# A two-layer hybrid attention kernel on one core: scores on 128 rows with stacked queries and doubled keys, norm steps in PSUM, stacked mixing weights

## The chip, the cores and the metric

The kernel runs on one core of one Trainium2 chip. Time is the device time of one execution in microseconds (us); the figure used is the median of several timed runs. A separate execution is recorded by the hardware profiler, and all rows of profiles come from that one. TensorE is called PE in the profile (its weight loads PEld), VectorE DVE, ScalarE ACT, GpSimd POOL, SyncE SP.

## The reference

512 tokens of width 1024 pass through two layers and a final RMS norm, all in float32. A layer, cut to what matters:

```python
h = rmsnorm(x, norm_g)                       # x * rsqrt(mean(x*x) + 1e-6) * g
proj = h @ w_in                              # all of what follows is a column range of proj
ya = moba_attention(rope(a_q), rope(a_k), a_v) * silu(a_g)         # 6 heads of 64, causal
yb = dsa_attention(rope(b_q), rope(b_k), b_v, rope(i_q), rope(i_k), i_w) * silu(b_g)
yc = dilated_mixture(rope(c_q), rope(c_k), c_v) * silu(c_g)        # 3 groups of 4 heads
merged = gate0 * (ya @ w_br_a) + gate1 * (yb @ w_br_b) + gate2 * (yc @ w_br_c)
x = x + merged @ w_out
```

Branch A (moba) is causal softmax attention at this length. Branch B (dsa) has six query heads over one key head, and attends for each token only to the 128 keys whose index score is highest; the index score is a weighted sum over four index heads of relu(iq . ik). Branch C has three groups of four heads with strides 1, 4 and 16; each group is attention within a band, and the three results of a head are mixed with weights from a softmax over their log-sum-exps.

## The kernel before, in words

**Products.** Every float32 product is made of three passes on TensorE. An operand is split into a high part (a cast on ScalarE) and a low part (a subtraction, on POOL for weights, tile `wlo`, line L326, and for operands from SBUF; on VectorE, L379, for operands from PSUM), and the passes are high x high, low x high and high x low. The projections (`t_block` L406, `n_block` L426) are such passes of 128 rows and up to 512 columns: lines L417 to L419 and L436 to L438.

**What sets the order.** The kernel first lists all its operations (`add`, L66), each with its engine, an assumed cost, the tiles that it reads and writes and a priority. `Plan.schedule` (L105) then lists them: at each step it takes, on the engine that can begin first, the operation that can begin first, and among those the one of the lowest priority number. A tile comes from a pool with a fixed number of slots by tag (for example two PSUM tiles for scores, "sc", and one, "pv", for the products with the values), and an operation that needs a new tile waits until a slot is free. Projections and branch products are "fill" (`pe_fill`, L339): they keep the order in which they are listed. Attention work has a lower priority number, so it goes ahead of fill as soon as its operands are there, and fill lies between its steps. The units of a layer are listed in the order of the string `ORDER` (L27): values, index, keys, top-k, queries, the branches' attention, gates, branch products. DMA transfers, weights and copies alike, are issued by SP's queue in the order of the plan (`dma`, L273).

**Queries and keys.** `rope_group` (L442) projects four heads at a time to 128-row tiles X and Y (the even and odd halves of four heads), rotates them on VectorE and POOL into tiles `rt`, and copies them by DMA to z tiles (`zq`, `zk`, `zn`, `zc` and so on), where two heads lie below one another, each on 64 rows. `split_pair` (L480) splits a z tile: a cast of 128x512 on ScalarE and a subtraction of 128x512 on POOL.

**Scores.** `scores` (L505) makes a block of scores, 128 queries by N keys (N is 128 to 512) of two heads: three products for two heads, six matmuls, each on 64 rows. The two heads of a pair use the two halves of the rows, and are issued one behind the other. There are 76 such blocks in the two layers: index (`topk`, L764), A and B (`attend`, L554) and group 0 of C (`c_group0`, L873). Groups 1 and 2 of C have their own code (L951, their scores in L963). `soft` (L520) and what follows it in `attend` make the softmax: mask, exponential and sum, reciprocal, the scaling by it (ScalarE, L586), transposes on TensorE (L591), the split, and the products with the values (`pv`, L614 and L626).

**Norm.** `square` (L636) sums the squares of a row tile (128 tokens) in four pieces, `rstd` (L705) makes 1/rms of it with four tiny VectorE steps on 128x1 or 128x4 (L712, L714 to L716) and a square root on ScalarE, all in one SBUF tile `sq`. `norm_tile` (L680) scales x by it and by the gain (`h`, L687; in layer 0 the gain is a PSUM tile `gp`, in layer 1 an SBUF tile `gb`), and TensorE transposes the result (`tpn`, L693). The final norm uses `rstd` too.

**Mixing.** `c_mix` (L1019) makes the weights of the three groups, transposes them to 12 rows, and splits them into `rh` and `rl`. For each of two head pairs and three groups a tile `bc` (L1057) spreads the weights of two heads over 128 rows: two matmuls of 12 rows, `sel` being a matrix of zeros and ones.

## Time and profile before

| | |
|---|---|
| median of 3 runs | 1096.1 us (1096.06 to 1096.89) |
| profiled execution, its own time | 1097.91 us |
| its span, first to last instruction | 1096.1 us |
| mean granted TensorE clock | 0.998 |
| instructions | 17334 |

The span is shorter than the profiled execution's own time by 1.8 us, which lie before its first and behind its last instruction. In the profile's rows a duration is that of one instruction as the profiler gives it; matmuls are pipelined, so that one begins before the row of the last has ended. A row of TensorE in the timeline that ends in "x2" stands for two matmuls that run side by side. In groups of instructions, what follows the second bar is the engine's idle time just before them, with what ended it.

### The profile page before, as it was taken

Reading aid. Unit: us, or ns where it says so; the run is one execution under the profiler, and the core shown is the slowest. Engines: PE = TensorE matmul, PEld = TensorE weight load, DVE = VectorE, ACT = ScalarE, POOL = GpSimd, SP = SyncE. Lnnn points to the kernel's source line nnn. Section 1 sums busy time; section 2 is a strip of 40 time slices with the busy share of each in tenths; the row PEclk is TensorE's granted clock in tenths of the full one; section 3 lists DMA queues with packets and bytes.
Section 4 is the critical chain, followed back from the end, with each engine's and each line's share of the span. In section 5 each row is a group of like instructions: output and inputs, shape, how many; then the busy total and the mean of one; then the engine's idle time right before and its main releaser. Section 6 shows DMA issues by size and latency. Waiting matters only on the chain.

```text
span 1096.1 us, 17334 instructions
## 1 busy us (share of the span) xinstructions
PE 1085.4 (99%) x5746; PEld 885.2 (81%) x5746; DVE 490.6 (45%) x1416; ACT 574.3 (52%) x1466; POOL 644.0 (59%) x656
## 2 busy tenths in 40 slices
PE   9999999999999999999999999999999999999997
PEld 5887887778878887888978788777888887778887
DVE  6127885465445313113351388755644452221144
ACT  5534336687767653334353343467876775532432
POOL 4764765654544637876566277565653455396853
PEclk9999999999999999999999999999999999999999
DMA  6642543523222332353654144434422224235322
GB/s 222 180 109 63 140 107 92 147 75 82 73 68 78 97 81 76 106 173 97 188 161 134 30 116 116 111 90 123 114 66 63 67 80 108 78 87 177 120 79 78
DMA packets 112596, 116.40 MB, mean 106 GB/s; under 512 B 17773, under 2 KB 94457, under 8 KB 112506
## 3 DMA queue, kind: packets, MB, share of 16 engines
q1 hardware_dynamic: 112216, 114.97, 37.8%
q8 instruction: 45, 0.74, 0.3%
q14 instruction: 45, 0.37, 0.1%
q10 hardware_dynamic: 290, 0.33, 0.1%
HBM read 96.06 MB, written 6.36 MB: 93 GB/s over the span
## 4 chain that ended last, share of the span: by engine, by line
PE 48%; DMA 1%; POOL 1%; issue 1%; ACT 1%; DVE 0%; SPq 0%; ACTq 0%
PE pp L417 11%; PE pp L419 11%; PE pp L418 11%; PE sc L515 2%; PE pp L436 2%; PE pp L438 1%; PE pp L437 1%; PE po L1112 1%; PE po L1111 1%; PE po L1110 1%; PE tp L591 1%; DMA ws<-in_w_in_dram 1%; PE pv L614 1%; PE pv L626 1%; POOL wlo L326 1%
## 5 line engine op out<-in xcount | busy, mean ns | idle before, releaser
L326 POOL TENSOR_TENSOR wlo<-ws,whi 128x256 fp32r<-128x256 f32 (+2 forms) x439 | 438.5, 1013 | 321.5 <-ACT whi L320 255.1
L417 PE MATMUL pp<-h_hi,whi 128*128 128x512 f32 (+1 forms) x896 | 361.8, 404 | 0.0
L419 PE MATMUL pp<-h_hi,wlo 128*128 128x512 f32 (+1 forms) x896 | 348.6, 389 | 0.0
L418 PE MATMUL pp<-h_lo,whi 128*128 128x512 f32 (+1 forms) x896 | 348.3, 389 | 0.0
L320 ACT CAST whi<-ws 128x512 fp32r<-128x512 f32 (+2 forms) x434 | 213.2, 507 | 250.0 <-PE pp L418 130.7
L417 PEld LDWEIGHTS pp<-h_hi,whi 128*128 128x128 f32 x896 | 168.4, 188 | 41.5 <-issue 7.4
L419 PEld LDWEIGHTS pp<-h_hi,wlo 128*128 128x128 f32 x896 | 168.2, 188 | 35.7
L418 PEld LDWEIGHTS pp<-h_lo,whi 128*128 128x128 f32 x896 | 168.7, 188 | 28.8
L379 DVE TENSOR_TENSOR ptl<-tp,pth 128x256 fp32r<-128x256 f32 (+3 forms) x128 | 58.0, 462 | 47.2 <-ACT pth L320 46.6
L847 DVE SCALAR_TENSOR_TENSOR th<-th,pp 128x512 f32<-128x512 f32 x32 | 22.0, 688 | 109.6 <-PE pp L419 106.7
L436 PE MATMUL pp<-whi,h_hi 128*128 128x512 f32 (+2 forms) x192 | 68.0, 354 | 0.0
L438 PE MATMUL pp<-whi,h_lo 128*128 128x512 f32 (+2 forms) x192 | 66.7, 348 | 0.0
L437 PE MATMUL pp<-wlo,h_hi 128*128 128x512 f32 (+2 forms) x192 | 66.7, 347 | 0.0
L320 ACT CAST pth<-tp 128x256 fp32r<-128x256 f32 (+3 forms) x128 | 50.3, 405 | 28.7 <-PE tp L591 18.2
L1110 PE MATMUL po<-whi,mhh 128*128 128x256 f32 (+1 forms) x192 | 61.4, 320 | 0.0
L1111 PE MATMUL po<-wlo,mhh 128*128 128x256 f32 (+1 forms) x192 | 61.1, 318 | 0.0
L1112 PE MATMUL po<-whi,mhl 128*128 128x256 f32 (+1 forms) x192 | 61.1, 318 | 0.0
L525 ACT ACTIVATE p<-p,st 128x128 f32<-128x128 f32 (+3 forms) x96 | 53.6, 559 | 3.1 <-DVE st L523 3.1
L832 ACT ACTIVATE th<-pp 128x512 f32<-128x512 f32 x48 | 28.6, 595 | 50.5 <-PE pp L419 50.3
L586 ACT ACTIVATE p<-p,st 128x128 f32<-128x128 f32 (+3 forms) x96 | 51.7, 558 | 1.9 <-DVE st L585 1.7
L417 PE MATMUL pp<-yh,whi 128*128 128x512 f32 x128 | 51.7, 404 | 0.0
L793 DVE MATCH_REPLACE8 work<-m,work 128x512 f32<-128x512 f32 (+2 forms) x96 | 51.6, 542 | 0.0
(198 smaller groups left out, 1718.4 us busy)
## 6 DMA issues: line engine op xcount, KB each, us to landing
ws<-in_w_in_dram SPq DMA_DIRECT2D x232, 256.0 KB, 2.9
ws<-in_w_out_dram SPq DMA_DIRECT2D x32, 256.0 KB, 2.7
ws<-in_w_in_dram SPq DMA_DIRECT2D x24, 192.0 KB, 2.8
zq<-rt SPq DMA_DIRECT2D x32, 128.0 KB, 2.8
x<-x SPq DMA_DIRECT2D x16, 256.0 KB, 3.5
x<-in_x_dram SPq DMA_DIRECT2D x15, 256.0 KB, 4.2
vd<-vn SPq DMA_DIRECT2D x8, 256.0 KB, 3.4
ws<-in_w_in_dram SPq DMA_DIRECT2D x16, 128.0 KB, 2.3
```

The lines of the kernel that those rows point to most:

```text
L320: add("act", n_act(n), lambda: nc.scalar.copy(dst(), src()), r=r, w=w, pri=pri, name=name, alt=("dve", n_dve(n, two), lambda: nc.vector.te ...
L326: add("pool", n_pool(n), lambda: nc.gpsimd.tensor_tensor(dst(), a(), b(), op), r=r, w=w, pri=pri, name=name, alt=("dve", n_dve(n), lambda: ...
L379: add("dve", n_dve(n), lambda: nc.vector.tensor_tensor(lo_fn(), src_fn(), hi_fn().bitcast(F32), ALU.subtract), r=[src, hi], w=[lo], pri=pr ...
L417: nc.tensor.matmul(o, lhs(hi.t, k % 2), a, start=(k == 0), stop=False)
L418: nc.tensor.matmul(o, lhs(hi.t, k % 2), b, start=False, stop=False)
L419: nc.tensor.matmul(o, lhs(lo.t, k % 2), a, start=False, stop=(k == nk - 1))
L436: nc.tensor.matmul(ps.t[:, :width], tokfn(h_hi, k), hi.t[:, kk, :width], start=(k == 0), stop=False)
L437: nc.tensor.matmul(ps.t[:, :width], tokfn(h_hi, k), lo.t[:, kk, :width], start=False, stop=False)
L438: nc.tensor.matmul(ps.t[:, :width], tokfn(h_lo, k), hi.t[:, kk, :width], start=False, stop=(k == KD - 1))
L1110: nc.tensor.matmul(ps.t[:, :n], mh.t[:, c], hi.t[:, kk, :n], start=(k == 0), stop=False)
L1111: nc.tensor.matmul(ps.t[:, :n], mh.t[:, c], lo.t[:, kk, :n], start=False, stop=False)
L1112: nc.tensor.matmul(ps.t[:, :n], ml.t[:, c], hi.t[:, kk, :n], start=False, stop=(k == KD - 1))
```

## The change

**Scores.** A query tile now holds one head: the high part on 64 rows and the low part on the other 64 (`split_heads`: a cast of 64x512 on ScalarE and a subtraction of 64x512 on VectorE for each head). A key tile holds one key head twice, on rows 0 to 63 and 64 to 127, and is split into high and low as before. Then the doubled key high part against the stacked query gives two products in one pass of 128 rows, and the doubled key low part against it gives the third, and low x low beside it. `scores` makes four matmuls of 128 rows where it made six of 64. It holds for the index, A, B and group 0 of C; groups 1 and 2 of C keep their 64 rows.

**Units.** Since the keys of A and of C's group 0 are stored twice, their rotation works on a pair of query heads and the same pair's key heads (`qk_a(p)`, `c_qk0(p)`), with a column of scale factors `scol` (-0.125 on the queries' rows, 1 on the keys') in place of one number or none. `twice` writes each key head by DMA to both halves of its tile, in pieces of 32 rows. The attention of A, B and C's group 0 is listed by pair (AA0 to AA2, AB0 to AB2, C00, C01), the rotations by pair (A0 to A2, D0, D1), C's group 0 values by themselves (CW), and `ORDER` is a new string.

**Norm.** The sums of squares of all four row tiles lie in one PSUM tile of tag "pv" (`Part` is eight columns of it). The tiny steps read it, and their results lie in an SBUF tile `rstd`. In layer 1 ScalarE writes the gain to PSUM tiles. The warm-up matmuls use the tag "pp". The four memsets of `sq` on POOL are one on VectorE in each layer's norm.

**Mixing.** High and low weights lie in one tile `rw` of 64 rows (rows 0 to 11 and 32 to 43, POOL sets the others to zero), `sel` has its ones on both, and `bc` is one matmul of 64 rows.

In all, over the whole program, TensorE has 5476 matmuls for 5640, VectorE 38 instructions more, ScalarE 35 more, POOL 20 fewer, and SP 672 transfers for 569.

The diff, cut to its core (`attend` loses its loop over pairs and is otherwise only moved to the left):

```diff
-ORDER = "CV I K V Q T gA C0 gB A AB VR AA C1 gC B1 C2 B0 MX B2"
+ORDER = "CV K I V Q D0 D1 A1 CW T gC C01 gA C00 gB A0 AB0 AB1 AB2 AA0 AA1 VR C1 A2 AA2 B1 C2 B0 MX B2"
...
+class Part:
+    def __init__(self, buf, at, tok):
+        self.buf, self.at, self.tok = buf, at, tok
+    @property
+    def t(self):
+        return self.buf.t[:, self.at:self.at + 8]
...
-        dma(lambda g=g, s32=s32: s32.t[4 * g:4 * g + 4], lambda: k_sel[32:36], s32, 300, pri=50)
+        for p0 in (4 * g, 32 + 4 * g):
+            dma(lambda s32=s32, p0=p0: s32.t[p0:p0 + 4], lambda: k_sel[32:36], s32, 300, pri=50)
...
-    warm = buf("pv", [P, T], F32, "warm")
+    warm = buf("pp", [P, T], F32, "warm")
...
+    def split_heads(z, name, t0=0):
+        out_ = []
+        pri = -5e4 + fill[1] + 0.5
+        n = T - t0
+        for f in range(2):
+            b = buf("u", [P, T], FR, name)
+            r, o = slice(64 * f, 64 * f + 64), slice(64 - 64 * f, 128 - 64 * f)
+            copy(n, lambda b=b, r=r: b.t[r, t0:], lambda r=r: z.t[r, t0:], [z], [b], pri, "hi", True)
+            add("dve", n_dve(n), lambda b=b, r=r, o=o: nc.vector.tensor_tensor(b.t[o, t0:], z.t[r, t0:], b.t[r, t0:].bitcast(F32), ALU.subtract),
+                r=[z], w=[b], pri=pri, name="lo", port=True)
+            out_.append(b)
+        return out_
...
     def scores(qp, kp, i, N, koff, name):
-        (qh, ql), (kh, kl) = qp, kp
         sc = [buf("sc", [P, T], F32, "sc") for _ in range(2)]
         pri = apri()
         def fn():
-            for n, (a, b) in enumerate(((qh, kh), (ql, kh), (qh, kl))):
-                for f in range(2):
-                    r = slice(64 * f, 64 * f + 64)
-                    nc.tensor.matmul(sc[f].t[:, :N], a.t[r, i * P:(i + 1) * P], b.t[r, koff:koff + N],
-                                     start=(n == 0), stop=(n == 2))
-        add("pe", n_pair(6, N), fn, r=[qh, ql, kh, kl], w=sc, pri=pri, name=name)
+            for f in range(2):
+                for n in range(2):
+                    nc.tensor.matmul(sc[f].t[:, :N], qp[f].t[:, i * P:(i + 1) * P], kp[f][n].t[:, koff:koff + N],
+                                     start=(n == 0), stop=(n == 1))
+        add("pe", n_mm(4, N), fn, r=[*qp, *kp[0], *kp[1]], w=sc, pri=pri, name=name)
         return sc, pri
...
-            sq[t] = buf("st", [P, 8], F32, "sq")
-            add("pool", 70, lambda st=sq[t]: nc.gpsimd.memset(st.t[:, 0:4], 0.0), w=[sq[t]], pri=-5e5, after=() if wide else plan.ops[-1:])
+            if t == 0:
+                stats[0] = buf("pv", [P, 32], F32, "sq")
+                add("dve", 80, lambda b=stats[0]: nc.vector.memset(b.t, 0.0), w=[stats[0]], pri=-5e5, after=() if wide else plan.ops[-1:])
+            sq[t] = Part(stats[0], 8 * t, token(f"sq{t}"))
...
+    def load_g(src, to_psum=False):
         g = [buf("u", [P, T], F32, "gb") for _ in range(2)]
         for b in range(2):
             dma(lambda b=b: g[b].t, lambda b=b: src[:, b * T:(b + 1) * T].to_broadcast([P, T]), g[b], 725, pri=-2e5, after=fills[-30:-29])
+        o = [buf("sc", [P, T], F32, "gp") for _ in range(2)] if to_psum else g
         for b in range(2):
-            add("act", n_act(T), lambda b=b: nc.scalar.activation(g[b].t, g[b].t, AF.Copy, scale=-0.5), r=[g[b]], w=[g[b]], pri=-2e5, name="gb",
-                alt=("dve", n_dve(T, True), lambda b=b: nc.vector.tensor_scalar(g[b].t, g[b].t, -0.5, None, op0=ALU.mult), 0.0), port=True)
-        return g
+            add("act", n_act(T), lambda b=b: nc.scalar.activation(o[b].t, g[b].t, AF.Copy, scale=-0.5), r=[g[b]], w=[o[b]], pri=-2e5, name="gb")
+        return o
...
-        st = sq[t]
-        rstd(st, pri)
+        st = rstd(sq[t], pri)
...
-                h.t[:, c], xb.t, st.t[:, 7:8], gb.t, op0=ALU.mult, op1=ALU.mult), r=[xs[t][b], st, gb[b]], w=[h], pri=pri, name="hn", port=port)
+                h.t[:, c], xb.t, st.t[:, 1:2], gb.t, op0=ALU.mult, op1=ALU.mult), r=[xs[t][b], st, gb[b]], w=[h], pri=pri, name="hn")
...
     def rstd(st, pri):
         c = lambda n: st.t[:, n:n + 1]
         stt = nc.vector.scalar_tensor_tensor
-        def tiny(fn, r=()):
-            add("dve", 80, fn, r=[st, *r], w=[st], pri=pri, name="tiny")
+        r = buf("st", [P, 8], F32, "rstd")
+        def tiny(fn, reads=(), w=None):
+            add("dve", 120, fn, r=[st.buf, *reads], w=[st.tok if w is None else w], pri=pri, name="tiny")
         tiny(lambda: nc.vector.tensor_tensor_reduce(st.t[:, 0:4], st.t[:, 0:4], invd.t, 1.0, EPS, ALU.mult, ALU.add, c(4)), [invd])
-        add("act", 250, lambda: nc.scalar.activation(c(5), c(4), AF.Sqrt), r=[st], w=[st], pri=pri, name="sqrt")
-        tiny(lambda: nc.vector.reciprocal(c(6), c(5)))
-        tiny(lambda: stt(c(5), c(6), c(6), c(4), op0=ALU.mult, op1=ALU.mult))
-        tiny(lambda: stt(c(7), c(5), -3.0, c(6), op0=ALU.add, op1=ALU.mult))
+        add("act", 250, lambda: nc.scalar.activation(c(5), c(4), AF.Sqrt), r=[st.buf], w=[st.tok], pri=pri, name="sqrt")
+        tiny(lambda: nc.vector.reciprocal(r.t[:, 0:1], c(5)), [st.tok], r)
+        tiny(lambda: stt(c(6), c(4), r.t[:, 0:1], r.t[:, 0:1], op0=ALU.mult, op1=ALU.mult), [r])
+        tiny(lambda: stt(r.t[:, 1:2], c(6), -3.0, r.t[:, 0:1], op0=ALU.add, op1=ALU.mult), [st.tok], r)
+        return r
...
-        gb = load_g(norm_g[l:l + 1, :]) if l else first_g()
+        gb = load_g(norm_g[l:l + 1, :], True) if l else first_g()
...
-            iq = [split_pair(z, "iq", t0=P) for z in zi]
+            iq = [split_heads(z, "iq", P) for z in zi]
...
-            bq2, bk, ik = split_pair(zb, "bq"), split_pair(zk, "bk"), split_pair(zn, "ik")
+            bq2, bk, ik = split_heads(zb, "bq"), split_pair(zk, "bk"), split_pair(zn, "ik")
...
-                    sc, pri = scores(iq[pr], ik, i, N, 0, "idx")
+                    sc, pri = scores(iq[pr], (ik, ik), i, N, 0, "idx")
...
-        def qk_a():
-            zq = [buf("z", [P, T], F32, "zq") for _ in range(2)]
-            rope_group(l, [(A_Q, 256)], -0.125, 1, [(0, 2, [(zq[0], 0)]), (2, 2, [(zq[1], 0)])], "aq")
-            aq = [split_pair(z, "aq") for z in zq]
...
+        def twice(zs, h0=0):
+            return [(h0 + n, 1, [(z, 0), (z, 64)]) for n, z in enumerate(zs)]
...
+        def qk_a(p):
+            zq = [buf("z", [P, T], F32, "zq") for _ in range(3)]
+            rope_group(l, [(A_Q + p * P, P), (A_K + p * P, P)], "scol", 1, [(0, 2, [(zq[0], 0)])] + twice(zq[1:], 2), "aqk")
+            R["aq"][p] = split_heads(zq[0], "aq")
+            R["ak"][p] = [split_pair(z, "ak") for z in zq[1:]]
...
+        def c_qk0(p):
+            z = [buf("z", [P, T], F32, "zc") for _ in range(3)]
+            rope_group(l, [(C_Q + p * P, P), (C_K + p * P, P)], "scol", 1, [(0, 2, [(z[0], 0)])] + twice(z[1:], 2), "c")
+            c0[p] = split_heads(z[0], "cq"), [split_pair(b, "ck") for b in z[1:]]
...
-                    sc, pri = scores(q[pr], k[pr], i, N, (i - nb + 1) * P, "scC")
+                    sc, pri = scores(q, k, i, N, (i - nb + 1) * P, "scC")
...
-            rh, rl = buf("u", [P, T], FR, "rh"), buf("u", [P, T], FR, "rl")
-            split(lambda: tp.t[0:12].rearrange("p b n -> p (b n)"), tp, lambda: rh.t[0:12], rh, lambda: rl.t[0:12], rl, T, pri, True)
+            rw = buf("u", [P, T], FR, "rw")
+            add("pool", n_pool(T) / 2, lambda: nc.gpsimd.memset(rw.t[0:64].bitcast(F32), 0.0), w=[rw], pri=pri, after=plan.ops[-1:])
+            split(lambda: tp.t[0:12].rearrange("p b n -> p (b n)"), tp, lambda: rw.t[0:12], rw, lambda: rw.t[32:44], rw, T, pri, True)
...
-                        for n in range(2):
-                            nc.tensor.matmul(bc.t, sel.t[0:12, 2 * g + pr, :], (rh, rl)[n].t[0:12], start=(n == 0), stop=(n == 1))
-                    add("pe", n_mm(2, T), fb, r=[rh, rl, sel], w=[bc], pri=pri, name="bc")
+                        nc.tensor.matmul(bc.t, sel.t[0:64, 2 * g + pr, :], rw.t[0:64], start=True, stop=True)
+                    add("pe", n_mm(1, T), fb, r=[rw, sel], w=[bc], pri=pri, name="bc")
```

On TensorE, the block of index scores of width 384 for one pair of index heads in layer 0. Tiles `sc` are the scores, `ikh` and `ikl` the index key's parts, `iqh`, `iql` the queries' parts before, `iq` the stacked query of one head after, `pp` a projection. Before:

```order
L419 MATMUL pp_930<-h_hi,wlo_720 128x512
L515 MATMUL sc_983<-ikh_902,iqh_773 128x384
L515 MATMUL sc_984<-ikh_902,iqh_773 128x384
L515 MATMUL sc_983<-ikh_902,iql_787 128x384
L515 MATMUL sc_984<-ikh_902,iql_787 128x384
L515 MATMUL sc_983<-ikl_910,iqh_773 128x384
L515 MATMUL sc_984<-ikl_910,iqh_773 128x384
L417 MATMUL pp_993<-h_hi,whi_661 128x512
```

And after:

```order
L430 MATMUL pp_958<-h_hi,wlo_657 128x512
L540 MATMUL sc_973<-ikh_863,iq_893 128x384
L540 MATMUL sc_973<-ikl_872,iq_893 128x384
L540 MATMUL sc_974<-ikh_863,iq_899 128x384
L540 MATMUL sc_974<-ikl_872,iq_899 128x384
L428 MATMUL pp_958<-h_hi,whi_669 128x512
```

Two matmuls fewer stand between the projections, and each score tile is now made of two that follow one another. Of the 76 blocks 42 now follow a projection matmul, 30 follow transposes and four a product with the values.

On VectorE, the norm of the second row tile in layer 0 (`sq` its sums, `x` the rows, `gp` the gain, `h_lo` the low part of the transposed rows). Before:

```order
L714 RECIPROCAL sq_97<-sq_97 128x1
L715 SCALAR_TENSOR_TENSOR sq_97<-sq_97 128x1
L379 TENSOR_TENSOR h_lo<-tpn_172,h_hi 128x4x128
L716 SCALAR_TENSOR_TENSOR sq_97<-sq_97 128x1
L687 SCALAR_TENSOR_TENSOR h_223<-x_124,sq_97,gp_140 128x512
```

And after:

```order
L738 RECIPROCAL rstd_181<-sq_93 128x1
L709 SCALAR_TENSOR_TENSOR h_164<-x_91,rstd_148,gp_141 128x512
L739 SCALAR_TENSOR_TENSOR sq_93<-sq_93,rstd_181 128x1
L740 SCALAR_TENSOR_TENSOR rstd_181<-sq_93,rstd_181 128x1
L390 TENSOR_TENSOR h_lo<-tpn_171,h_hi 128x4x128
L709 SCALAR_TENSOR_TENSOR h_215<-x_118,rstd_181,gp_134 128x512
```

The last tiny step now stands ahead of the low part that it followed, and a half of the first tile's `h` stands behind the reciprocal.

On SP's queue, the copies for group 0 of C in layer 0 (`zc` the z tiles, `rt` the rotated tiles, `ws` weights). Before, four copies make two query pairs:

```order
L274 DMA ws_1415<-in_w_in_dram 128x2x256
L274 DMA zc_1426<-rt_1334 64x512
L274 DMA zc_1429<-rt_1334 64x512
L274 DMA zc_1426<-rt_1400 64x512
L274 DMA zc_1429<-rt_1400 64x512
L274 DMA ws_1471<-in_w_in_dram 128x2x256
```

After, two copies of 64 rows make one query pair, and eight of 32 rows its two key heads; the first of these two key heads is shown:

```order
L284 DMA zc_1265<-rt_1172 64x512
L284 DMA ws_1269<-in_w_in_dram 128x2x256
L284 DMA ws_1279<-in_w_in_dram 128x2x256
L284 DMA zc_1265<-rt_1240 64x512
L284 DMA zc_1305<-rt_1172 32x512
L284 DMA zc_1305<-rt_1240 32x512
L284 DMA zc_1305<-rt_1172 32x512
L284 DMA zc_1305<-rt_1240 32x512
L284 DMA ws_1337<-in_w_in_dram 128x2x256
```

The key copies stand between weight loads, and the weight loads of the next unit stand behind them.

More of the change, by code (lines that the diff above doesn't have):

```diff
@@ L379, in split @@
             add("dve", n_dve(n), lambda: nc.vector.tensor_tensor(lo_fn(), src_fn(), hi_fn().bitcast(F32), ALU.subtract),
-                r=[src, hi], w=[lo], pri=pri, name="lo")
+                r=[src, hi] if hi is not lo else [src], w=[lo], pri=pri, name="lo")
         else:
@@ L858, in branch @@
                 products(s - 1)
-        U = []
+        U = {}
         V0 = []
@@ L867, in c_qk, with c_values0 @@
             for c, s in ((C_Q, -0.125), (C_K, None)):
-                z = [buf("u" if g else "z", [P, T], F32, "zc") for _ in range(2)]
+                z = [buf("u", [P, T], F32, "zc") for _ in range(2)]
                 rope_group(l, [(c + g * 256, 256)], s, perm, [(0, 2, [(z[0], 0)]), (2, 2, [(z[1], 0)])], "c")
-                sc_.append(z if g else [split_pair(b, "c") for b in z])
+                sc_.append(z)
             return sc_
-        def c_group0():
-            q, k = c_qk(0, 1)
+        c0 = [None] * 2
+        U0 = [None] * 2
+        def c_qk0(p):
+            z = [buf("z", [P, T], F32, "zc") for _ in range(3)]
+            rope_group(l, [(C_Q + p * P, P), (C_K + p * P, P)], "scol", 1, [(0, 2, [(z[0], 0)])] + twice(z[1:], 2), "c")
+            c0[p] = split_heads(z[0], "cq"), [split_pair(b, "ck") for b in z[1:]]
+        def c_values0():
             sec = section([(C_V, 256)], w_in[l])
@@ L882, in c_group0 @@
                       lambda v0=v0: v0.t[:, :, 0:64], v0, lambda v0=v0: v0.t[:, :, 64:128], v0, 256, pri, True)
-            us = []
-            for pr in range(2):
+        def c_group0(pr):
+            us, (q, k) = U0, c0[pr]
+            if True:
                 pth = [buf("pt", [P, 8, P], FR, "pth") for _ in range(2)]
@@ L926, in c_group0 @@
                         r=[pv, tmp], w=[u], pri=pri, name="yadd")
-            U.append(us)
+            U[0] = us
         VR = []
@@ L1071, in layer @@
         units = {
-            "V": values, "I": index_qk, "K": keys_b, "T": topk, "Q": queries_b, "A": qk_a,
+            "V": values, "I": index_qk, "K": keys_b, "T": topk, "Q": queries_b,
+            **{f"A{p}": lambda p=p: qk_a(p) for p in range(3)}, **{f"D{p}": lambda p=p: c_qk0(p) for p in range(2)},
+            **{f"AA{p}": lambda p=p: R["yA"].__setitem__(p, attend("A", l, p, R["aq"][p], R["ak"][p], V, R["gA"], None)) for p in range(3)},
+            **{f"AB{p}": lambda p=p: R["yB"].__setitem__(p, attend("B", l, p, R["bq"][p], (R["bk"], R["bk"]), V, R["gB"], R["masks"])) for p in range(3)},
+            **{f"C0{p}": lambda p=p: c_group0(p) for p in range(2)}, "CW": c_values0,
             "gB": lambda: R.update(gB=gate_blocks(l, B_G, 3)), "gA": lambda: R.update(gA=gate_blocks(l, A_G, 3)),
             "gC": lambda: R.update(gC=gate_blocks(l, C_G, 2)),
-            "AB": lambda: R.update(yB=attend("B", l, R["bq"], R["bk"], V, R["gB"], R["masks"])),
-            "AA": lambda: R.update(yA=attend("A", l, R["aq"], R["ak"], V, R["gA"], None)),
-            "C0": c_group0, "CV": c_values, "VR": load_values, "C1": lambda: c_group(1), "C2": lambda: c_group(2), "MX": lambda: R.update(yC=c_mix(R["gC"])),
+            "CV": c_values, "VR": load_values, "C1": lambda: c_group(1), "C2": lambda: c_group(2), "MX": lambda: R.update(yC=c_mix(R["gC"])),
             "B1": lambda: branch(1, R["yB"], w_br_b, 3, ORDER.split()[-1] == "B1"),
```

171 lines of the change are left out of this document (79 added, 92 removed).

## The prediction

> **What bounds the kernel now.** I read the page first: the share of each engine, then the chain of work that ended last.
>
> ```profile
> span 1096.1 us, 17334 instructions
> PE 1085.4 (99%) x5746; PEld 885.2 (81%) x5746; DVE 490.6 (45%) x1416; ACT 574.3 (52%) x1466; POOL 644.0 (59%) x656
> PE 48%; DMA 1%; POOL 1%; issue 1%; ACT 1%; DVE 0%; SPq 0%; ACTq 0%
> ```
>
> TensorE is busy for 99% of the span, the other engines for 45 to 59%, and the chain that ends last runs on TensorE wherever it is followed (48% against 1% for each other). But a busy row on PE is not PE at its peak, since the ends of its rows are modelled. So I go by the distance from one start to the next, in the timeline. Here is a score block of width 512 (two heads, three products, so three pairs, each shown as one row "x2") between projection matmuls. The columns are start, duration, engine, line.
>
> ```profile
> 83.87 0.39 PE L418 MATMUL pp<-h_lo,whi 128*128 128x512 f32 x1
> 84.10 0.39 PE L419 MATMUL pp<-h_hi,wlo 128*128 128x512 f32 x1
> 84.42 0.50 PE L515 MATMUL sc<-ikh,iqh 64*128 64x512 f32 x2
> 84.75 0.40 PE L515 MATMUL sc<-ikh,iql 64*128 64x512 f32 x2
> 84.98 0.39 PE L515 MATMUL sc<-ikl,iqh 64*128 64x512 f32 x2
> 85.31 0.50 PE L417 MATMUL pp<-h_hi,whi 128*128 128x512 f32 x1
> 85.64 0.40 PE L418 MATMUL pp<-h_lo,whi 128*128 128x512 f32 x1
> ```
>
> A projection matmul takes 0.23 (83.87 to 84.10), and so does an undisturbed pair (84.75 to 84.98). So two heads on the two row halves do share one pass. The other steps are longer: 0.32 into the block, 0.33 for its first pair, 0.33 out of it, 0.33 for the first projection matmul behind it. These four are some 0.10 above 0.23 each, so a block pays about 0.4 us beside its passes. I measure a block from the last projection start ahead of it to the second one behind it, less two ordinary pitches: 85.64 - 84.10 - 0.46 = 1.08.
>
> **The scores, part by part.** The same measure for the narrower blocks:
>
> ```profile
> 92.55 0.40 PE L419 MATMUL pp<-h_hi,wlo 128*128 128x512 f32 x1
> 92.87 0.39 PE L515 MATMUL sc<-ikh,iqh 64*128 64x256 f32 x2
> ...
> 93.76 0.40 PE L418 MATMUL pp<-h_lo,whi 128*128 128x512 f32 x1
> ```
>
> ```profile
> 195.15 0.40 PE L419 MATMUL pp<-h_hi,wlo 128*128 128x512 f32 x1
> ...
> 196.29 0.39 PE L418 MATMUL pp<-h_lo,whi 128*128 128x512 f32 x1
> ```
>
> Width 256 is the first of the two, width 128 (a block of branch B in between) the second: 1.21 - 0.46 = 0.75 and 1.14 - 0.46 = 0.68. For 384 I take the middle of 512 and 256, 0.92 (an estimate). After the change a block is four matmuls of 128 rows. The trace has 128-row matmuls of narrow width among the products with the values:
>
> ```profile
> 309.25 0.40 PE L419 MATMUL pp<-h_hi,wlo 128*128 128x512 f32 x1
> 309.49 0.28 PE L614 MATMUL pv<-pth,v 128*128 128x256 f32 x1
> 309.60 0.28 PE L614 MATMUL pv<-ptl,v 128*128 128x256 f32 x1
> 309.72 0.22 PE L614 MATMUL pv<-pth,v 128*128 128x128 f32 x1
> 309.78 0.27 PE L614 MATMUL pv<-ptl,v 128*128 128x128 f32 x1
> 309.89 0.45 PE L417 MATMUL pp<-h_hi,whi 128*128 128x512 f32 x1
> ```
>
> There is no step into them (309.25 to 309.49 is an ordinary 0.24). One of width 256 takes 0.11 to 0.12; I use 0.115. Those of width 128 show 0.06 and 0.11 to the next start; I price each at 0.115, like the second, and keep 0.06 for the range. Width 384 is estimated midway between 0.23 and 0.115, at 0.17. Four passes then cost 0.92, 0.68, 0.46 and 0.46 for 512, 384, 256 and 128, and a block gains 0.16, 0.24, 0.29 and 0.22. How many blocks there are stands in the answer on the scores' line; each block has two matmuls of its first product, so the counts are halved:
>
> ```profile
> L515 PE MATMUL sc<-bkh,bqh x48: 322/411/501, 195.5 to 787.9; 64*128 64x128 f32 x12, 64*128 64x256 f32 x12, 64*128 64x384 f32 x12, 64*128 64x512 f32 x12
> L515 PE MATMUL sc<-akh,aqh x48: 322/412/497, 259.3 to 882.7; 64*128 64x128 f32 x12, 64*128 64x256 f32 x12, 64*128 64x384 f32 x12, 64*128 64x512 f32 x12
> L515 PE MATMUL sc<-ch,ch x32: 322/381/385, 150.9 to 725.5; 64*128 64x256 f32 x24, 64*128 64x128 f32 x8
> L515 PE MATMUL sc<-ikh,iqh x24: 381/440/498, 80.6 to 630.2; 64*128 64x512 f32 x8, 64*128 64x384 f32 x8, 64*128 64x256 f32 x8
> ```
>
> That makes 16 blocks of 512, 16 of 384, 28 of 256 and 16 of 128, 76 in all. Gain: 16 x 0.16 + 16 x 0.24 + 28 x 0.29 + 16 x 0.22 = 2.6 + 3.8 + 8.1 + 3.5 = 18.0 us. One part of it may not be had. In the new order 30 of the 76 blocks stand right behind transposes, and a 128-row matmul there is slowed as well:
>
> ```profile
> 892.55 0.66 PE L591 MATMUL tp<-ident,p 128*128 128x128 f32 x4
> 892.96 0.48 PE L417 MATMUL pp<-h_hi,whi 128*128 128x512 f32 x1
> 893.27 0.39 PE L418 MATMUL pp<-h_lo,whi 128*128 128x512 f32 x1
> ```
>
> It took 0.31 instead of 0.23. If a score block inherits the slowdown its gain shrinks by up to 0.08; half of that for 30 blocks is 1.2 us. The scores leave 16.8, on TensorE, which sets the end.
>
> The Trainium skill speaks against this step: "TensorEngine Tiling (Array Packing)", section "Performance Considerations" (When to Use Tiling), has a contraction of 64 split into two row tiles, which is what the kernel before does and the change gives up. By it alone the four full passes lose against three shared ones; the trace shows the sharing (0.23 for a pair) and also the 0.4 that it costs to enter and leave. That cost agrees with the page's "Key Properties", by which a change of the tiling mode drains the array.
>
> **The mixing weights.** Their passes have 12 rows:
>
> ```profile
> 962.05 0.39 PE L1057 MATMUL bc<-rh,sel 12*128 12x512 f32 x1
> 962.29 0.38 PE L1057 MATMUL bc<-rl,sel 12*128 12x512 f32 x1
> ```
>
> One costs 0.24 here. Two layers x two pairs x three groups are 12 broadcasts, each with one pass less: 12 x 0.24 = 2.9 us. They stay in a part of the array (64 rows), so their entry cost is not counted as saved. The memset of the stacked tile is queued on POOL behind the weights' low parts, and the split's two halves on ScalarE and VectorE wait for it; the mixing has branch projections beside it on TensorE, so I cost it at nothing. Without that cover it costs one POOL instruction on the way (about the 1.27 of a subtraction, quoted next).
>
> **The norm.** TensorE waits at the transposes of the normalized rows; the first row has its idle time behind the second bar, and then what ended it.
>
> ```profile
> L693 PE MATMUL tpn<-ident,h 128*128 128x128 f32 x64 | 10.3, 285 | 2.5 <-DVE h L687 2.2 <-DVE sq L714 0.3
> 13.68 1.27 POOL L326 TENSOR_TENSOR wlo<-ws,whi 128x512 fp32r<-128x512 f32 x1 [3.09 <-ACT whi L320]
> 13.72 1.24 DVE L716 SCALAR_TENSOR_TENSOR sq<-sq 128x1 f32<-128x1 f32 x1
> 1091.11 0.16 DVE L716 SCALAR_TENSOR_TENSOR sq<-sq 128x1 f32<-128x1 f32 x1
> ```
>
> All of that idle time is 2.5 us, most of it behind DVE's h. One reason is in the two rows that follow: a step on one column took 1.24 while POOL subtracted beside it, and 0.16 at the tail with POOL idle. After the change the tiny steps have their running values in PSUM, and layer 1's gain lies there too. The trace has no such step, so I bound it: 2.5 if all idle goes, -0.3 if the steps become as much longer as they now hold TensorE (the 0.3 behind sq). I take 1.8, nearer the upper end because the 1.24 against 0.16 is most of a wait of this size.
>
> The Trainium skill, "SBUF — State Buffer", section "Who interferes with whom", says that VectorE and GpSimd exclude each other on a shared port, which VectorE needs for a second input from SBUF. The 1.24 us row agrees; by the rule the whole 2.5 would go, by the rows as I weigh them 1.8.
>
> **What is late next.** The softmax chain that hides under TensorE's work keeps its length while the work over it shrinks by 0.16 to 0.29 us a block. The tightest place that I found:
>
> ```profile
> 793.23 0.62 ACT L586 ACTIVATE p<-p,st 128x384 f32<-128x384 f32 x1
> 794.10 0.49 PE L591 MATMUL tp<-ident,p 128*128 128x128 f32 x3
> ```
>
> ScalarE ends at 793.85, the transposes begin at 794.10: 0.25 to spare. At six places like it I lose the whole 0.25, 1.5 us; none is the one bound, all 76 blocks (19 us) the other. The change also adds 103 transfers to SP's queue (672 for 569), since key heads are written twice in 32-row pieces:
>
> ```profile
> SPq L274 <- POOL wlo L326: 688.2, 306, 17.7
> L274 SPq DMA_DIRECT2D zk<-rt x8: 547/592/683, 69.0 to 607.3; - x8
> ```
>
> An issue of that piece holds SP for 0.59 us, so 103 cost it 61 us at most, and its 688 us of waiting for the weights' buffers take that up on average. Not everywhere: units D0, D1 and A1 follow one another, with 3 x (10 copies + 8 weight loads) = 54 issues, at 0.59 each 32 us, against 3 x 48 projection matmuls of 0.23 = 33 us on TensorE. Weights queue behind copies that wait for POOL's rope there. It just fits, so I cost it at nothing, and rival one takes it up. VectorE gets 36 subtractions more and POOL 20 instructions less; with VectorE at 45% these lie beside TensorE's work.
>
> **The sum.** 16.8 + 2.9 + 1.8 - 1.5 = 20.0 us. The profiled execution took 1097.9 (span 1096.1 and 1.8 around it), so it becomes 1077.9; the median of the runs, 1096.1, lies 1.8 below the profiled time, so I forecast 1076 for it. With the two bounded terms at their nearer ends (norm 0 to 2.5, stalls 0 to 5) this case reaches from 1072 to 1081.
>
> **Rivals.**
> One: stalls give half back. The 0.25 of slack is gone at 40 of the 76 blocks, 10 us, or weights come late behind the copies by as much at the three units in each layer. For it speaks the thin margin of 32 against 33 us; against it that the order is listed anew and TensorE has projection matmuls to put between. Time: 1096.1 - 10 = about 1086; I say 1085.
>
> Two: slower. The 0.4 us at a block's ends may not come from the 64 rows but from the turn to another kind of work, as behind transposes, which have 128 rows and yet slow the next matmul by 0.08. Then it stays, and the block has one more pass: 16 x 0.23 + 16 x 0.17 + 44 x 0.115 = 11.5 us. Less 2.9 and 1.8 that is 6.8 slower, 1103. It decides from the point where less than one pass's worth (0.115 to 0.23) of the 0.4 goes. Against it: the narrow products with the values are another kind of work too, and TensorE goes into them at 0.24 and through them at 0.115. By the tiling rule named above the result would be this one.
>
> Three: more gain. The blocks behind transposes lose nothing (18.0), all the norm's idle goes (2.5), nothing stalls, and width 128 runs at the 0.06 seen at 309.72: 16 x 4 x 0.055 = 3.5 more. 18.0 + 2.9 + 2.5 + 3.5 = 26.9, or 1069.
>
> **How the numbers follow.** My forecast has a chance of 0.68, rival one 0.17, rival two 0.07, rival three 0.08. The range runs from 1069 (rival three) to 1087 (rival one with 1 us of margin); rival two, and the tails beyond, are the 2 in 10 left out. Faster by over 0.2% (2.2 us, what a measurement here can tell from no change) are the forecast and rivals three and one, less a little for a stall loss near the whole gain: 0.90; within it 0.03; slower 0.07, rival two.
>
> **What would show it.** In the timeline of the changed kernel a score block of 512 should have steps near 0.23 throughout, one of 256 near 0.115, and no 0.33 behind it when it stands between projections; steps of 0.33 would show rival two. TensorE's busy time should fall by about 18 to 20 us, with its idle time unchanged or smaller; a larger idle time before transposes, or waits of TensorE on weights between 100 and 200 us, would show rival one. Idle time before tpn should fall below 1 us. The forecast is wrong if the blocks gain what they should and the span does not.

## The result and the profile after

The change makes the kernel faster: 1077.95 us (1076.92 to 1080.07, 4 runs) against 1096.49, a ratio of 0.9836 with a 95% interval of 0.9822 to 0.9851; that is 18.5 us between the medians and 18.0 by the ratio. Measured a second time, beside new runs of the kernel before, it was 1077.69 against 1094.88, a ratio of 0.9842 (0.9828 to 0.9857), 17.2 us. The forecast was 1076 in a range of 1069 to 1087.

The profiled execution took 1077.46, 20.4 less than the one before (1097.91). Its page, first the span, then the engines:

```profile
span 1075.7 us, 17326 instructions
PE 1064.6 (99%) x5582; PEld 896.4 (83%) x5582; DVE 513.2 (48%) x1454; ACT 594.8 (55%) x1501; POOL 635.9 (59%) x636
```

TensorE still sets the end: the chain that ended last runs on it for 93% of the span. Its busy time fell by 20.8 us (1085.4 to 1064.6). The trace counts 5582 matmuls where the one before has 5746: two fewer in each of the 76 blocks, and 12 broadcasts fewer. VectorE and ScalarE are some 20 us busier each, most of it beside TensorE's work. In the timeline a score block now looks like this, one of width 512 between projections of width 452, and one of 256 between projections of 512:

```profile
78.26 0.37 PE L449 MATMUL pp<-whi,h_lo 128*128 128x452 f32 x1
78.47 0.39 PE L540 MATMUL sc<-ikh,iq 128*128 128x512 f32 x1
78.70 0.40 PE L540 MATMUL sc<-ikl,iq 128*128 128x512 f32 x1
78.94 0.39 PE L540 MATMUL sc<-ikh,iq 128*128 128x512 f32 x1
79.17 0.40 PE L540 MATMUL sc<-ikl,iq 128*128 128x512 f32 x1
79.40 0.37 PE L447 MATMUL pp<-whi,h_hi 128*128 128x452 f32 x1
79.60 0.37 PE L448 MATMUL pp<-wlo,h_hi 128*128 128x452 f32 x1
...
87.36 0.39 PE L430 MATMUL pp<-h_hi,wlo 128*128 128x512 f32 x1
87.59 0.28 PE L540 MATMUL sc<-ikh,iq 128*128 128x256 f32 x1
...
88.06 0.39 PE L428 MATMUL pp<-h_hi,whi 128*128 128x512 f32 x1
88.29 0.39 PE L429 MATMUL pp<-h_lo,whi 128*128 128x512 f32 x1
```

No step is longer than an ordinary pass: 0.23 for each of the four of 512, (88.06 - 87.59) / 4 = 0.12 for each of 256, and the first projection behind the block takes its ordinary 0.20 or 0.23. The 0.33s of before are gone. Adding up, over all score blocks of each trace, the time from their first start to the next other matmul, and what the neighbours on both sides took beyond an ordinary pass, gives 63.6 us before and 49.0 after: 14.6 us.

TensorE's wait for normalized rows is gone too. The first row is the last tiny step of the kernel before, the others are of the change (columns as before: busy and mean, then idle time of the engine):

```profile
L716 DVE SCALAR_TENSOR_TENSOR sq<-sq 128x1 f32<-128x1 f32 x12 | 5.1, 423 | 0.4
L715 PE MATMUL tpn<-ident,h 128*128 128x128 f32 x64 | 10.1, 282 | 0.1
L740 DVE SCALAR_TENSOR_TENSOR rstd<-sq,rstd 128x1 f32<-128x1 f32 x12 | 1.9, 155 | 0.3
```

The idle time before the transposes fell from 2.5 to 0.1 us. The last tiny step takes 155 ns in the mean instead of 423; one of the 423's steps is the 1.24 us beside POOL that the prediction quotes. And `h` takes 740 ns in the mean over both layers, where the trace before has 743 in layer 0 and 926 in layer 1.

What TensorE waits for now, outside the start, is above all ScalarE's emptying of a projection tile (us in total, times, longest):

```profile
PE pp L428 <- ACT th L856: 1.7, 3, 0.9
```

Each of the two long ones is a gap of about 1.0 to 1.2 us in TensorE's starts, in branch A of each layer (at 300.6 and 828.3). Rows of all engines around the first and the second show why:

```profile
300.30 0.38 ACT L558 ACTIVATE gj<-sc 128x256 f32<-128x256 f32 x1 [1.38 <-DVE y L574]
...
301.18 0.59 ACT L856 ACTIVATE th<-pp 128x512 f32<-128x512 f32 x1
...
301.82 0.50 PE L428 MATMUL pp<-h_hi,whi 128*128 128x512 f32 x1 [0.87 <-ACT th L856]
...
305.10 1.28 DVE L871 SCALAR_TENSOR_TENSOR mg<-th,pp 128x512 f32<-128x512 f32 x2 [0.39 <-PE sc L540]
...
828.74 0.60 ACT L856 ACTIVATE th<-pp 128x512 f32<-128x512 f32 x1 [1.40 <-PE pp L430]
...
831.31 1.28 DVE L871 SCALAR_TENSOR_TENSOR mg<-th,pp 128x512 f32<-128x512 f32 x2 [0.59 <-PE sc L540]
```

The kernel has three projection tiles. At both places two of them hold finished branch products, which VectorE merges (`mg`) only at 305.10 and 831.31, behind the gap. The third is the projection that has just ended, and TensorE stands still until ScalarE has emptied it (`th`). In the first gap `th` also begins some 0.2 us late: it is queued behind the guard on the scores (`guard`, tile `gj`, a throw-away output that shares four slots with the branch outputs), which waited 1.38 us for VectorE's `y` to free a slot. In the second ScalarE is idle for 1.40 before `th`, and TensorE still waits 0.69 for it. The rows of the merges show them released by a score matmul; a merge writes a tile of the tag "u", which the parts of queries and keys use too, so it may wait for one of their slots, but no run tests that. The third wait, near the end, has `th` behind the scaling of the final norm's gain on ScalarE, which waits 2.23 for its DMA.

So the 20.4 us of the two profiled executions divide into 14.6 for the scores, 2.8 for the mixing (the six blocks of broadcasts took 8.0 and take 5.2), 3.4 for the starts that were late at normalized rows, less 2.6 for the three new gaps outside score blocks (the two above and 0.45 at 993): 18.2. The other 2.2 are spread over many small steps. Some 0.8 of them is a matter of counting: three score blocks now pay a step behind other matmuls that three projections paid before (below). The rest was not traced to a cause.

### The profile page after: what moved, and what is told of

Same layout as the page of the kernel before. It is cut to its first block, busy times and chain, and to the rows that moved or that the text cites. A ratio compares the mean times of both kernels' runs of the same rounds, so it can differ in the third digit from the quotient of the medians.

```text
span 1075.7 us, 17326 instructions
## 1 busy us (share of the span) xinstructions
PE 1064.6 (99%) x5582; PEld 896.4 (83%) x5582; DVE 513.2 (48%) x1454; ACT 594.8 (55%) x1501; POOL 635.9 (59%) x636
## 4 chain that ended last, share of the span: by engine, by line
PE 93%; DMA 2%; issue 1%; POOL 1%; ACT 1%; DVE 1%; ACTq 0%; SPq 0%; POOLq 0%; DVEq 0%
PE pp L428 22%; PE pp L429 21%; PE pp L430 21%; PE sc L540 4%; PE pp L449 3%; PE pp L447 3%; PE pp L448 3%; PE tp L612 2%; PE pv L635 1%; POOL wlo L337 1%; PE po L1147 1%; PE po L1148 1%; PE po L1149 1%; PE pv L647 1%; DMA ws<-in_w_in_dram 1%
## 5 line engine op out<-in xcount | busy, mean ns | idle before, releaser
L428 PE MATMUL pp<-h_hi,whi 128*128 128x512 f32 (+1 forms) x896 | 356.8, 398 | 2.1 <-ACT th L856 1.7
L331 ACT CAST whi<-ws 128x256 fp32r<-128x256 f32 (+2 forms) x436 | 215.9, 508 | 238.4 <-PE pp L429 117.5
L818 DVE MATCH_REPLACE8 work<-m,work 128x512 f32<-128x512 f32 (+2 forms) x96 | 51.8, 543 | 0.1
```

What stands on the lines that cost most here:

```text
L331: add("act", n_act(n), lambda: nc.scalar.copy(dst(), src()), r=r, w=w, pri=pri, name=name, alt=("dve", n_dve(n, two), lambda: nc.vector.te ...
L428: nc.tensor.matmul(o, lhs(hi.t, k % 2), a, start=(k == 0), stop=False)
```

## The experiments

"Before" is always the kernel before, run on the same chip. Where a run is compared with the change on a chip where the change itself was not run, the change is taken as 0.984 of that "before".

**What costs 0.4 us at a block's ends: 64 rows cut out of the change.** Edit of the changed kernel:

```diff
-                    nc.tensor.matmul(sc[f].t[:, :N], qp[f].t[:, i * P:(i + 1) * P], kp[f][n].t[:, koff:koff + N],
+                    nc.tensor.matmul(sc[f].t[:, :N], qp[f].t[0:64, i * P:(i + 1) * P], kp[f][n].t[0:64, koff:koff + N],
```

> The changed kernel with its four score passes cut to the upper 64 rows of the stacked query and the doubled key; the products of the other 64 rows are left out. Same instructions in the same order, same number of passes. Theory (the cost at a block's ends comes from 64 rows beside 128): about 0.4 us comes back at most of the 76 blocks, 25 to 30 us, so 1103 to 1108 us; blocks of 512 between projections go from 0.91 to about 1.3. Rival (it comes from the turn to another kind of work): nothing changes, 1078.

Measured: 1104.34 us against 1095.20 before, ratio 1.0084 (1.0067 to 1.0101); the change on that chip is about 1077.6, so 27 us slower. The timeline at the index's second block of 512:

```profile
79.34 0.37 PE L449 MATMUL pp<-whi,h_lo 128*128 128x452 f32 x1
79.64 0.50 PE L540 MATMUL sc<-ikh,iq 64*128 64x512 f32 x1
79.98 0.39 PE L540 MATMUL sc<-ikl,iq 64*128 64x512 f32 x1
80.22 0.39 PE L540 MATMUL sc<-ikh,iq 64*128 64x512 f32 x1
80.44 0.39 PE L540 MATMUL sc<-ikl,iq 64*128 64x512 f32 x1
80.77 0.47 PE L447 MATMUL pp<-whi,h_hi 128*128 128x452 f32 x1
81.08 0.37 PE L448 MATMUL pp<-wlo,h_hi 128*128 128x452 f32 x1
```

Four steps are 0.10 longer again: into the block (0.30 for a pass of 452 that takes 0.20), through its first pass (0.34), out of it (0.33), and through the first projection behind (0.31 for 0.20). Nothing but the row count differs from the change. Over all blocks the sum is 75.5 against 49.0 us, 26.5 more, which is the time. The rival, a cost of turning to another kind of work, falls.

**What the pairing was worth: six full passes in the kernel before.** Edit:

```diff
-                    r = slice(64 * f, 64 * f + 64)
+                    r = slice(0, 128)
                     nc.tensor.matmul(sc[f].t[:, :N], a.t[r, i * P:(i + 1) * P], b.t[r, koff:koff + N],
```

> The kernel before with each of its six score matmuls a block on all 128 rows instead of 64; each score is then a sum over both heads of the pair, which no run needs. Theory: no step at the ends, but six full passes, blocks of 1.38, 1.02, 0.69 and 0.69 us for 512, 384, 256 and 128 against 1.09, 0.92, 0.75 and 0.685 measured before: +4.8 +1.6 -1.7 +0.1 = about 5 us slower than before, 1101. Rival (the ends cost 0.4 whatever the rows): six full passes and the ends, some 30 us more, 1131.

Measured: 1100.34 against 1095.20, ratio 1.0052 (1.0037 to 1.0067): 5.1 us slower, as the theory had it.

```profile
84.63 0.39 PE L419 MATMUL pp<-h_hi,wlo 128*128 128x512 f32 x1
84.86 0.62 PE L515 MATMUL sc<-ikh,iqh 128*128 128x512 f32 x2
85.31 0.62 PE L515 MATMUL sc<-ikh,iql 128*128 128x512 f32 x2
85.76 0.61 PE L515 MATMUL sc<-ikl,iqh 128*128 128x512 f32 x2
86.22 0.39 PE L417 MATMUL pp<-h_hi,whi 128*128 128x512 f32 x1
```

A pair on 128 rows takes 0.45, twice a pass, and no step at the ends is left. All blocks together take 69.7 us against 63.6 before: pairing saves three passes in six and gives back 0.4 for each block. At 512 and 384 it wins (1.09 against 1.37, 0.93 against 1.06); at 128 the two are even (0.68), and at 256 it loses (0.75 against 0.72).

**The broadcasts on 128 rows.** Edit of the changed kernel:

```diff
-            add("pool", n_pool(T) / 2, lambda: nc.gpsimd.memset(rw.t[0:64].bitcast(F32), 0.0), w=[rw], pri=pri, after=plan.ops[-1:])
+            add("pool", n_pool(T) / 2, lambda: nc.gpsimd.memset(rw.t.bitcast(F32), 0.0), w=[rw], pri=pri, after=plan.ops[-1:])
-                        nc.tensor.matmul(bc.t, sel.t[0:64, 2 * g + pr, :], rw.t[0:64], start=True, stop=True)
+                        nc.tensor.matmul(bc.t, sel.t[:, 2 * g + pr, :], rw.t, start=True, stop=True)
```

> The changed kernel with the mixing broadcasts on all 128 rows (the added rows are zeros). Theory: the six blocks of two broadcasts lose their steps in and out, 0.20 us each, so 1.2 us faster than the changed kernel, about 1076.7, and a block of two takes 0.46 between projections instead of 0.66. Rival: as it is, 1078.

Measured: 1075.75 against 1095.20, ratio 0.9824 (0.9809 to 0.9839), which is 1.9 us below the 1077.6 of the change there, with overlapping intervals. In the timeline the effect is plain. The first block of two broadcasts, in the change:

```profile
414.10 0.39 PE L430 MATMUL pp<-h_hi,wlo 128*128 128x512 f32 x1
414.41 0.73 PE L1092 MATMUL bc<-rw,sel 64*128 64x512 f32 x2
415.07 0.50 PE L428 MATMUL pp<-h_hi,whi 128*128 128x512 f32 x1
415.41 0.40 PE L429 MATMUL pp<-h_lo,whi 128*128 128x512 f32 x1
```

and with 128 rows:

```profile
414.32 0.40 PE L430 MATMUL pp<-h_hi,wlo 128*128 128x512 f32 x1
414.56 0.62 PE L1092 MATMUL bc<-rw,sel 128*128 128x512 f32 x2
415.02 0.40 PE L428 MATMUL pp<-h_hi,whi 128*128 128x512 f32 x1
415.25 0.39 PE L429 MATMUL pp<-h_lo,whi 128*128 128x512 f32 x1
```

A block falls from 0.86 to 0.48, since the whole 0.4 goes; the expectation had counted two of the four steps. Six such blocks make 2.3 us. Here rows of zeros are cheaper than rows left out.

**The guard's own tile.** Edit of the changed kernel, which also adds one slot for the new tag:

```diff
-        junk = buf("yt", [P, 256], F32, "gj")
+        junk = buf("gj", [P, 256], mybir.dt.bfloat16, "gj")
```

> The changed kernel with a buffer of its own (bfloat16) for the throw-away output of the guard on ScalarE, which shared the four slots of the branch output tiles. Theory: TensorE's two waits of 1.15 and 0.97 us in branch A of the two layers, where ScalarE held back the emptying of a projection tile because the guard waited for a slot, go away: 2.1 us faster, about 1076. Rival: another operation on ScalarE is late in its place, and the time stays within 0.5 us of 1078.

Measured: 1075.56 against 1095.20, ratio 0.9821 (0.9807 to 0.9836), 2.0 below the change, again with overlapping intervals. Both gaps in branch A are gone, and so is ScalarE's wait for a slot. But the planner listed everything anew with the new tag, and the order differs on all engines. VectorE's merges now stand ahead of the place where TensorE needs the tiles, in the first layer at 296.66 and in the second at 821.29 and 822.68:

```profile
296.66 1.29 DVE L871 SCALAR_TENSOR_TENSOR mg<-th,pp 128x512 f32<-128x512 f32 x2 [0.47 <-PE sc L540]
```

So the run shows that the two gaps can be won back. It does not show that the guard's wait made them, as the expectation says; by the rows of the change it accounts for 0.2 us. The wait near the end is left, and its gap grew from 0.45 to 1.15, so the trace has 1.4 of the 2.0.

**Both together.** Edit: the two above.

> The changed kernel with the mixing broadcasts on 128 rows and the guard's own buffer together. If both gain what was expected of each, 1.2 + 2.1 = 3.3 us faster than the changed kernel: about 1074.7. Rival: neither moves the end, 1078.

Measured: 1073.34 against 1095.38, ratio 0.9795 (0.9782 to 0.9808). That is 4.5 below the change (1077.8 on that chip), with intervals that no longer overlap, and near the sum of the two, 3.9. TensorE is busy for 1061.8 of a span of 1071.1 us.

**The parts alone: scores, norm, mixing.** The changed kernel with norm and mixing as before; the kernel before with the norm's part; the kernel before with the mixing's part. The core of the first; the other two make the opposite edits in the kernel before:

```diff
-            sq[t] = Part(stats[0], 8 * t, token(f"sq{t}"))
+            sq[t] = buf("st", [P, 8], F32, "sq")
...
-                        nc.tensor.matmul(bc.t, sel.t[0:64, 2 * g + pr, :], rw.t[0:64], start=True, stop=True)
+                        for n in range(2):
+                            nc.tensor.matmul(bc.t, sel.t[0:12, 2 * g + pr, :], (rh, rl)[n].t[0:12], start=(n == 0), stop=(n == 1))
```

> The changed kernel with the norm and the mixing as before: scores, units and order alone. By the prediction: 16.8 gained less 1.5 of new stalls, 1081. By the trace after (score blocks 14.6 less, new stalls of about 2.6 outside them): 1084 to 1085, of which the rest to 1078 is norm (3.4) and mixing (2.8). Rival: the parts don't add, and this alone is within 1 us of 1078.

> The kernel before with the norm's part of the change alone (sums and tiny steps in PSUM, layer 1's gain in PSUM, warm-up matmuls on the other tag). By the prediction 1.8 us faster (1094.6); by the trace after, in which the waits of TensorE for normalized rows are gone (3.4 us in all), 1093. Rival: the waits go to another place and the time is as before, 1096.4.

> The kernel before with the mixing's part of the change alone. By the prediction 12 x 0.24 = 2.9 us faster, 1093.6. Rival: the tile's memset on POOL comes late and TensorE waits for the broadcasts, so no gain, 1096.4.

Measured against 1095.38: scores 1088.65, ratio 0.9932 (0.9917 to 0.9947), 6.7 faster; norm 1093.86, ratio 0.9984 (0.9975 to 0.9992), 1.5 faster; mixing 1091.76, ratio 0.9966 (0.9954 to 0.9978), 3.6 faster. Norm and mixing are near what was expected. The scores alone miss both expectations (1081 and 1084 to 1085), and the three together make 11.8 of some 17.5 us. Two things are in the trace of the scores alone. One is a gap of 3.0 us at 159 us, told below. The other is the granted clock, which here fell for ten microseconds:

```profile
core 0: us, PE busy (x) PEld busy (x) DVE busy (x) ACT busy (x) POOL busy (x), PEclk, DMA share, GB/s
424.00:434.00 10.00, 10.00 (x23) 6.12 (x22) 3.17 (x5) 1.15 (x3) 7.45 (x8) 0.51 0.21 53
```

At 0.51 the ten microseconds hold five microseconds of work. The six runs of this kernel go with the clock that was granted: 1085.9 and 1087.0 at means of 0.999 and 0.995, 1087.4 to 1090.2 at 0.989 to 0.993. By the two runs at 0.995 and above the scores alone are worth about 9 us (an estimate). That is what 14.6 for the blocks, less 2.6 for the gaps and 3.0 for this one, gives.

**Norm undone, mixing undone, and the change again.** The changed kernel with only the norm, or only the mixing, as before (the edits above, one at a time), and the change itself beside them.

> The changed kernel with the norm as before. By the trace after (no waits of TensorE for normalized rows, 3.4 us before): about 3 us slower than the changed kernel, ratio to before near 0.986. Rival (the norm alone was worth 1.5 us, and the score units were 8 to 9 us short in the run without norm and mixing because a stall appears with the old norm's list order): 6 us or more slower, ratio 0.989 or more.

> The changed kernel with the mixing weights as before (two broadcasts of 12 rows). By the trace: 2.8 us slower than the changed kernel, ratio to before near 0.986. Rival (the list order changes with it, and a stall like the one of 3.1 us at 159 us in the run of the scores alone appears): 6 us or more slower.

> The changed kernel itself, on the chip of these runs, to compare them with. Ratio to before 0.982 to 0.985 as in the first measurement, some 18 us faster than before.

Measured against 1094.88: norm undone 1083.13, ratio 0.9895 (0.9878 to 0.9911); mixing undone 1080.36, ratio 0.9873 (0.9858 to 0.9888); the change 1077.69. So the mixing is worth 2.7 us in place, as the trace said. Undoing the norm costs 5.4, between its two expectations, and its trace has the same gap as the scores alone had. First TensorE's rows, then VectorE's:

```profile
159.69 0.39 PE L430 MATMUL pp<-h_hi,wlo 128*128 128x512 f32 x1
162.90 0.42 PE L540 MATMUL sc<-ckh,cq 128*128 128x256 f32 x1 [2.83 <-DVE mixt L548]
```

```profile
161.16 1.48 DVE L818 TENSOR_SCALAR work<-work 128x512 f32<-128x512 f32 x3
162.56 0.28 DVE L548 CUSTOM_DVE_ANT_0 p<-sc,band 128x128 f32<-128x128 f32 x1
```

The scores of C's group 0 wait for a free score tile, and the mask that frees it (`p<-sc,band`) stands on VectorE behind the last steps of the top-k and its masks (L818). In the change the same masks stand between the top-k steps. The gap, 3.0 us, thus comes from the place of four instructions in VectorE's list, which the planner chose otherwise with the old norm. Right behind it the granted clock fell as well (columns as in the row of the scores alone, the clock third from the end):

```profile
162.90:166.40 3.50, 3.50 (x16) 3.01 (x17) 2.52 (x13) 2.92 (x12) 0.00 (x0) 0.53 0.17 37
```

That is some 1.7 us more. At the normalized rows this trace has one late start, of 0.7 us, where the trace before has 3.4. So most of the 5.4 is the other list and what followed from it, and what the norm's steps are worth by themselves in the changed kernel is not shown. With 5.4 and 2.7 taken from the scores alone at an undisturbed clock (1086.5), 1078.4 is left, near the 1077.7 of the whole.

**SP's queue: each key copy issued twice.** Edit of the changed kernel, for the key heads of A and of C's group 0; the instructions of all other engines stay in the same order:

```diff
+                    if m == 1 and name in ("aqk", "c"):
+                        def two(b=b, p0=p0, half=half, s=s, h=h):
+                            for e in range(2):
+                                nc.sync.dma_start(b.t[p0 + 32 * e + half:p0 + 32 * e + 32:2, t0:], s.t[32 * h + 16 * e:32 * h + 16 * e + 16, t0:])
+                        add("sp", 650, two, r=[s], w=[b], pri=pri, lag=1900.0)
+                        continue
```

> The changed kernel with each of the 80 copies of 32 rows of a key head issued as two copies of 16 rows; the order on all other engines is the same. It doubles the cost of the doubled keys on SP's queue, at 0.59 us an issue 47 us more in all, 4.7 us more in each unit of two heads. Theory (SP has slack, its 619 us of waiting for weight buffers): within 1 us of the changed kernel. Rival (the queue is just full around units D0, D1 and A1, and weights come late): at least 5 of the 14 us added there in each layer are paid, 10 us slower, about 1087.

Measured: 1083.92, ratio 0.9899 (0.9884 to 0.9914), 6.2 us slower than the change. Neither expectation holds. Most of the 47 us of added issues is taken up (the queue's waits for the weights' buffers fall from 617 to 581 us), but not all. What is late are not the weights. The first row is a wait of TensorE, the second one of ScalarE:

```profile
PE tp L943 <- ACT p L556: 3.5, 3, 1.5
153.27 0.62 ACT L331 CAST akh<-zq 128x512 fp32r<-128x512 f32 x1 [3.99 <-DMA zq<-rt]
```

TensorE waits at transposes of softmax rows, 3.5 us in C's group 0 and 1.3 in A, and two waits of 0.9 for the stacked query and the key's low part of C's group 0 come with them. The second row shows how for the longest of them: ScalarE's cast of A's next keys waits 3.99 us for their copies, and the softmax of C's group 0 is queued behind it. The copies that arrive late are those of the heads that attend next.

## Why the prediction was right, and where not

**The scores' mechanism was right.** The 0.4 us at a block's ends belongs to the 64 rows (26.5 us come back with them), passes of 128 rows cost what the projections and the products with the values cost, and the fourth pass is paid out of that. Blocks between projections gained 0.19, 0.21, 0.27 and 0.24 for 512, 384, 256 and 128, against 0.16, 0.24, 0.29 and 0.22. The term of 16.8 measured 14.6. What it lacked is not the 1.2 for blocks behind transposes: those cost as much as the others (0.48 at 256 in both places). The pass behind the transposes does take 0.08 longer, but it also begins 0.08 sooner: the last transpose is followed after 0.03, where the others take 0.11. It lacked, in each layer, the first block of the head pair of C's group 0 that is listed second. It is 128 wide and costs 0.75 and 1.84 instead of 0.45, because TensorE waits there for score tiles (in layer 1) and, behind the block, for a projection tile (in both). And it lacked three blocks in A behind products with the values of C's other groups, which fill 64 of the columns and after which a step of 0.15 and a longer first pass are paid, some 0.26 a block. These 0.8 us are the ones that projections paid before.

**The rule on row tiles** that spoke against the change (Trainium skill, "TensorEngine Tiling (Array Packing)", "Performance Considerations") agrees with the wide blocks, where six full passes cost 1.37 and the tiled pairs 1.09 (width 512). In this kernel the tiled pairs are no gain at 256 and 128 between 128-row work, nor against four stacked passes at any width. Rival two, which would have followed it, fell with the first run.

**The mixing** measured 2.8 in the trace and 2.7 in place, for a term of 2.9. That the steps at its ends stay was right; they are 0.4 a block, and the 128-row run took them out.

**The norm's term of 1.8 was too small by the trace**: the idle row fell from 2.5 to 0.1, the whole upper bound. That bound is what the Trainium skill's rule on the shared port ("SBUF — State Buffer", "Who interferes with whom") gave. Timed alone the norm is worth 1.5 (interval 0.9 to 2.7), which does not tell 1.8 from 2.5. In that run's trace one late start of 0.45 is left at the normalized rows, and its first projection begins 0.8 later than before (15.80 against 15.04); why the medians differ by no more than 1.5 is not shown beyond that.

**The stalls' term of 1.5 was too small and its mechanism wrong.** The softmax chain that was to lose its 0.25 us of slack does not appear among TensorE's waits after: none is at transposes of softmax rows. The new gaps, 2.6 us outside the blocks, come where TensorE has no free projection tile: at the two long ones two of the three wait for VectorE's merges, and at the third ScalarE is held by the final norm's gain. That a throw-away output's slot stands behind the two long ones was expected of the run with the guard's own tile, and that run does not show it.

**SP's queue at nothing** was right for the change, and the margin was wider than the 32 against 33 us said: doubling the key copies adds 14 us of issues at those units in each layer and costs 6.2 in both together. The prediction named late weights as the danger; what came late were the copies themselves.

**The offset failed.** The sum, 1077.9 for a profiled execution, met 1077.46. The step from there to the median took 1.8 us off, because the profiled execution before lay 1.8 above its median. That distance belonged to one execution and not to the kernel: the change's profiled execution lies 0.5 below its own median. So the gain of 20 was 20.4 between the two profiled executions and 17.2 to 18.5 between medians, and the forecast was 2 us low.

**Luck had a part in the sum.** That it met the profiled execution within 0.4 us comes from errors that cancel: against the trace the scores were 2.2 too high, the stalls 1.1 too kind and the norm 1.6 too low (its late starts took 3.4), and 2.2 that no term names came on top.

## What to carry to other kernels

Count what it costs to enter and to leave a matmul of fewer rows from the start-to-start distances of its neighbours, on both sides of the block, before believing that two tiles side by side are a gain; here short blocks between full-height work were better off with all 128 rows filled, with a second part of the operand or, in the mixing, even with zeros. When parts of a change are timed alone on a kernel that a planner lists, look for the waits that the new list made, or took away, before calling the difference the part's worth. A difference of two profiled executions is not a difference of medians: an offset of one execution should not be carried over to the next kernel.

## What had not been expected of the hardware

The cost of 64-row work beside 128-row work is the same 0.10 us at four places (into, first pass, out, first pass behind), with pairs of heads on both halves, with single passes on one half, and with 12 rows or 64 rows of the mixing. And TensorE's granted clock fell to about half in the middle of three of the fourteen profiled executions, with about 1.00 before and behind: for some ten microseconds with the scores alone, for 6.8 from 950.6 with the mixing undone, and for 3.4 with the norm undone. The last of these falls came right behind TensorE's idle gap of 2.8 us. The other two began among the broadcasts of 12 rows; the three other traces with such broadcasts show no fall there, and what set these two off was not found.
